# Scores of the chunked gated linear attention: seven halvings of the block in place of three quarterings, with the diagonal taken by itself

## The chip, the cores and the metric

The kernel is a single program on 1 of the cores of one Trainium2 chip. The metric is device microseconds of that core for one execution; what counts is the median over several runs. All data are 32-bit floats.

## The reference, cut to what matters

One layer of a hybrid decoder trunk over 256 tokens of width 2048. The normalised input goes through one wide projection. Three branches read it: gated linear attention (GLA), a softmax attention with a forgetting bias (FoX) and a cross-attention into 256 memory tokens. Their outputs are gated, projected, summed and projected once more. The change lies in the first branch, which has 4 heads with 128 key channels each:

```python
def step(state, inp):
    qi, ki, vi, gi = inp
    b = jnp.cumsum(gi, axis=2)
    ...
    diff = b[:, :, :, None, :] - b[:, :, None, :, :]
    decay = jnp.exp(jnp.where(causal[None, None, :, :, None], diff, -jnp.inf))
    scores = jnp.einsum('bhid,bhjd,bhijd->bhij', qi, ki, decay)
    o_intra = jnp.einsum('bhij,bhje->bhie', scores, vi)
```

A score of query i and key j is a sum over 128 channels d of q[i,d] · k[j,d] · exp(b[i,d] − b[j,d]), for j ≤ i. The decay depends on the channel, so the scores are no plain matrix product. Where a fixed token m lies between the keys and the queries, the factor splits into exp(b[i]−b[m]) · exp(b[m]−b[j]), both at most 1, and a matrix product over the channels does it.

## The kernel before, in words

**The stream of weights.** Nearly all of the work is a chain of matrix products with 2048 x 512 blocks of weights, taken in the order of the list `ORDER` (lines 39 to 46): GLA queries, keys, two value blocks, FoX queries, keys, values, memory keys, and so on to the output projection. A block comes in four loads of 1 MB on SyncE's queue (`w_load`, three buffers `raw`). ScalarE casts each eighth of a block to a rounded part `hi` (`w_cast`, L174), VectorE takes the rest `lo` = raw − `hi` (`w_sub`, L187), and TensorE multiplies by both. Of `hi` and of `lo` there are four buffers each. A block is done either as `natural` (L224 to L226: tokens on the partitions of the result, three products of 512 columns per token half and 128 rows of weights) or as `transposed` (L254 and L259: features on the partitions, groups of four products of 512 columns and four of 256, one group per 128 features and quarter of the block).

**What sets the order.** The order is written by hand. The weight stream is the backbone; everything else is written as generators that stand in three lanes (`post`, `side`, `main`). After every piece of the stream (one group in `transposed`, six products in `natural`) `pull()` lets each lane emit up to its next `yield`; `yield n` means that the next n pulls are between this stage and the next. Engines work through their own instructions in this order.

**The scores.** `gla_scores` (L590 to L723) runs in the lane `main`, beside the blocks of FoX queries, keys and values and the start of the memory keys. The 4 heads times 256 tokens stand along the free axis as 8 blocks `e` of 128 tokens, 128 channels on the partitions. `gB` holds the cumulated log decay (L575), `gqf` and `gkf` queries and keys, and `gA` the 8 score blocks of 128 x 128, which start as zeros. The products between the first 128 tokens and the last 128 (`cd`, L666) and the output (`gla_out`, L725 and on, L736, L737) stay as they are.

Inside a block of 128 tokens it goes in three levels, s = 32, 8 and 2. At a level each run of 4s tokens falls into quarters. Every key is scaled once, relative to the end of its own quarter (`prep_keys`, L612; the exponential L678; times the keys L681). For each of the three quarter ends b the queries after it are scaled relative to it (`prep_queries`, L623, three subtractions per half of the blocks; the exponential L682 or L686; `times_q`, L631). The three sets stand side by side, 96 + 64 + 32 = 192 columns per block. TensorE multiplies the 128 keys of a block with its 192 columns of queries (L707), two blocks into one PSUM bank, four such banks per level. From each bank VectorE copies three parts into `gA` under a mask (`copy_predicated`, L721). A fourth round does the pairs of neighbours (`prep_pairs`, L641, L642, L698, L647) and the diagonal: its right-hand side is 64 columns of odd queries and 128 columns of plain queries, so that the same product of 192 columns gives both. Masks are made by GpSimd at the start (`make_masks`, L494).

In numbers: 32 products of 192 columns. Two of them are emitted between two pulls, so that they stand in 16 places of TensorE's order. Tiles of 4 KB per partition (`a4`) come from a pool of 14; the scores take 11 of them in the levels.

```python
            for c in range(4):
                ps = att()[:, :2 * Q_N].rearrange("p (a b) -> p a b", a=2)
                for j in range(2):
                    e = 2 * c + j
                    MM(ps[:, j, :], lhsT=E[:, e * P:(e + 1) * P], rhs=Qs[c // 2][:, e % 4, :],
                       start=True, stop=True)
                ...
                yield 1
                for dst, mask, src in places:
                    nc.vector.copy_predicated(
                        dst, mask.bitcast(U32).unsqueeze(1).to_broadcast(list(src.shape)), src)
            yield 1
```

Of the kernel before, what the change touches and what calls it, by code (L numbers as in the profile page):

```python
# [10 lines left out]
F32 = mybir.dt.float32  # L11
F32R = mybir.dt.float32r
AF = mybir.ActivationFunctionType
ALU = mybir.AluOpType
AX = mybir.AxisListType

P = 128
# [33 lines left out]
QS = 128 ** -0.5  # L51
N_WARM = 7

STEPS = (32, 8, 2)
Q_OFF = (0, 96, 160)
Q_N = 192
BR_KT = (range(0, 8), range(8, 12), range(12, 16))


# [1 line left out]
def body(ctx, tc, xw, memT, xn, memn, wall, wsm, wup, cst, fgain, out):  # L61
    nc = tc.nc
    MM = nc.tensor.matmul

    cpool = ctx.enter_context(tc.tile_pool(name="cpool", bufs=1))
# [16 lines left out]
    def a4(shape, dt=F32):  # L82
        return apool.tile(shape, dt, tag="a4", name=nm("a"))
# [7 lines left out]
    def att():  # L91
        return ps_att.tile([P, NB], F32, tag="att", name=nm("att"))
# [232 lines left out]
    def row_of(col, row, wait=2):  # L325

        dg = a2([P, NT, P])
        for t in range(NT):
# [16 lines left out]
    ident = cpool.tile([P, P], F32, name="ident")  # L345
    ones = cpool.tile([P, P], F32, name="ones")
    nc.vector.memset(ones, 1.0)
    nc.gpsimd.affine_select(out=ident, in_=ones, pattern=[[-1, P]],
                            compare_op=ALU.is_equal, fill=0.0, base=0,
                            channel_multiplier=1)  # L350
# [136 lines left out]
        return r  # L487


    gmask = cpool.tile([P, len(STEPS), Q_N], F32, name="gmask")  # L490
    gpair = cpool.tile([P, 64], F32, name="gpair")
    fmask = cpool.tile([P, 3 * P], F32, name="fmask")

    def make_masks():  # L494

        nc.gpsimd.memset(gmask, 1.0)
        for li, s in enumerate(STEPS):
            for b in range(3):
                w, nb = (3 - b) * s, 32 // s
                mk_ = gmask[:, li, Q_OFF[b]:Q_OFF[b] + nb * w].rearrange("p (b s) -> p b s", s=w)  # L500
                nc.gpsimd.affine_select(out=mk_, in_=mk_, pattern=[[-4 * s, nb], [0, w]],
                                        compare_op=ALU.is_ge, fill=0.0, base=-b * s, channel_multiplier=1)
                nc.gpsimd.affine_select(out=mk_, in_=mk_, pattern=[[4 * s, nb], [0, w]],
                                        compare_op=ALU.is_ge, fill=0.0, base=(b + 1) * s - 1, channel_multiplier=-1)

        nc.gpsimd.affine_select(out=gpair, in_=ones[:, :64], pattern=[[-2, 64]], compare_op=ALU.is_equal,
                                fill=0.0, base=0, channel_multiplier=1)

        nc.gpsimd.memset(fmask, 0.0)
        for c in (0, 2):  # L510
            nc.gpsimd.affine_select(out=fmask[:, c * P:(c + 1) * P], in_=fmask[:, c * P:(c + 1) * P],
                                    pattern=[[-1, P]], compare_op=ALU.is_ge, fill=-1e30,
                                    base=0, channel_multiplier=1)
# [76 lines left out]
    def gla_scores():  # L590
        gB, gq, gk = G["B"], G["q"], G["k"]
        gqf, gkf = gq.rearrange("p h s -> p (h s)"), gk.rearrange("p h s -> p (h s)")
        B4 = gB.rearrange("p (h t i) -> p h t i", h=4, t=2)

        def blocks(x, half, s):

            return x[:, 512 * half:512 * half + 512].rearrange("p (b s) -> p b s", s=s)

        def of_q(Q, b, s):
            w = (3 - b) * s  # L600
            return Q[:, :, Q_OFF[b]:Q_OFF[b] + 32 * (3 - b)].rearrange("p e (b s) -> p e b s", s=w)

        def later(x, half, b, s):

            v = blocks(x, half, 4 * s)[:, :, (b + 1) * s:]
            return v.rearrange("p (e b) s -> p e b s", e=4)

        def prep_keys(s):

            E = a4([P, 1024])  # L610
            Bv = gB.rearrange("p (b s) -> p b s", s=s)
            nc.vector.tensor_tensor(out=E.rearrange("p (b s) -> p b s", s=s),  # L612
                                    in0=Bv[:, :, s - 1:s].to_broadcast([P, 1024 // s, s]), in1=Bv,
                                    op=ALU.subtract)
            return E

        def prep_queries(s, half):

            Q = a4([P, 4, Q_N])
            for b in range(3):  # L620
                w, nb = (3 - b) * s, 32 // s
                end = blocks(gB, half, 4 * s)[:, :, (b + 1) * s - 1:(b + 1) * s]
                nc.vector.tensor_tensor(  # L623
                    out=of_q(Q, b, s), in0=later(gB, half, b, s),
                    in1=end.rearrange("p (e b) s -> p e b s", e=4).to_broadcast([P, 4, nb, w]),
                    op=ALU.subtract)
            return Q

        def times_q(Q, s, half):
            for b in range(3):  # L630
                nc.vector.tensor_tensor(out=of_q(Q, b, s), in0=of_q(Q, b, s),  # L631
                                        in1=later(gqf, half, b, s), op=ALU.mult)

        def pick(v, u):
            return v[:, :, u].rearrange("p (e b) -> p e b", e=4)

        def prep_pairs(half):

            Q = a4([P, 4, Q_N])
            Bh = blocks(gB, half, 2)  # L640
            nc.vector.tensor_tensor(out=Q[:, :, :64], in0=pick(Bh, 1), in1=pick(Bh, 0), op=ALU.subtract)  # L641
            nc.scalar.copy(Q[:, :, 64:], gqf[:, 512 * half:512 * half + 512].rearrange(  # L642
                "p (e i) -> p e i", e=4))
            return Q

        def times_odd(Q, half):
            nc.vector.tensor_tensor(out=Q[:, :, :64], in0=Q[:, :, :64],  # L647
                                    in1=pick(blocks(gqf, half, 2), 1), op=ALU.mult)


        gA = G["A"] = a4([P, 8, P])
        nc.gpsimd.memset(gA, 0.0)
        U32 = mybir.dt.uint32
        cd = a4([P, 4, 2, P])
        nc.vector.tensor_tensor(out=cd[:, :, 0, :], in0=B4[:, :, 0, P - 1:P].to_broadcast([P, 4, P]),
                                in1=B4[:, :, 0, :], op=ALU.subtract)
# [7 lines left out]
        ps = att()  # L664
# [4 lines left out]
        nc.scalar.copy(gX, ps.rearrange("p (a b) -> p a b", a=4))  # L669
        yield from fox_decay()  # L670

        for li in range(len(STEPS) + 1):
            s = STEPS[li] if li < len(STEPS) else None
            Qs = []
            if s:
                E = prep_keys(s)
                yield 2
                nc.scalar.activation(E, E, AF.Exp, scale=1.0 / 16)  # L678
                Qs.append(prep_queries(s, 0))
                yield 2  # L680
                nc.vector.tensor_tensor(out=E, in0=E, in1=gkf, op=ALU.mult)  # L681
                nc.scalar.activation(Qs[0], Qs[0], AF.Exp, scale=1.0 / 16)  # L682
                yield 2
                Qs.append(prep_queries(s, 1))
                yield 2
                nc.scalar.activation(Qs[1], Qs[1], AF.Exp, scale=1.0 / 16)  # L686
                times_q(Qs[0], s, 0)
                yield 2
                times_q(Qs[1], s, 1)
                yield 2  # L690
            else:
                E = gkf
                for half in range(2):
                    Qs.append(prep_pairs(half))
                yield 2
                for half in range(2):
                    odd = Qs[half][:, :, :64]
                    nc.scalar.activation(odd, odd, AF.Exp, scale=1.0 / 16)  # L698
                yield 2
                for half in range(2):  # L700
                    times_odd(Qs[half], half)
                yield 2
            for c in range(4):
                ps = att()[:, :2 * Q_N].rearrange("p (a b) -> p a b", a=2)
                for j in range(2):
                    e = 2 * c + j
                    MM(ps[:, j, :], lhsT=E[:, e * P:(e + 1) * P], rhs=Qs[c // 2][:, e % 4, :],  # L707
                       start=True, stop=True)
                A2 = gA[:, 2 * c:2 * c + 2, :]
                if s:  # L710
                    places = [(A2.rearrange("p a (b s) -> p a b s", s=4 * s)[:, :, :, (b + 1) * s:],
                               gmask[:, li, Q_OFF[b]:Q_OFF[b] + 32 * (3 - b)].rearrange(
                                   "p (b s) -> p b s", s=(3 - b) * s),
                               ps[:, :, Q_OFF[b]:Q_OFF[b] + 32 * (3 - b)].rearrange(
                                   "p a (b s) -> p a b s", s=(3 - b) * s)) for b in range(3)]
                else:
                    places = [(A2.rearrange("p a (b s) -> p a b s", s=2)[:, :, :, 1], gpair, ps[:, :, :64]),
                              (A2, ident, ps[:, :, 64:])]
                yield 1
                for dst, mask, src in places:  # L720
                    nc.vector.copy_predicated(  # L721
                        dst, mask.bitcast(U32).unsqueeze(1).to_broadcast(list(src.shape)), src)
            yield 1  # L723

    def gla_out():  # L725
        oa = G["o"] = [a4([P, 1024]) for _ in range(NT)]
# [301 lines left out]
    for n in range(4):  # L1028
        gates = []
        for br in range(3):  # L1030
            ps = natural(x12, range(KT), w_kts(w_block()))
# [201 lines left out]
```

## Time and profile before

| | |
|---|---|
| median of 3 runs | 810.99 us (810.86 to 811.27) |
| the profiled execution | 810.85 us |
| its span, first to last instruction | 808.8 us |
| TensorE matmul busy | 799.7 us, 99% of the span |
| TensorE weight load busy | 673.5 us, 83% |
| VectorE busy | 498.3 us, 62% |
| ScalarE busy | 404.6 us, 50% |
| GpSimd busy | 23.7 us, 3% |
| first and last product of the score levels start at | 108.7 and 186 us |

The profiled execution takes 2.05 us more than its span: that is what lies before the first and after the last instruction. Busy times of TensorE are of overlapping products: a row of the trace gives an instruction's own duration, and what one costs in a stream is the distance from its start to the next one's. A matrix product of 32-bit floats stands in the trace as two loads of weights and two matmuls; the products of the weight stream, in the rounded format, as one of each. A row of the timeline merges neighbours of one line, and its time is that from the first one's start to the last one's end.

### The profile page before, as it was taken

How to read it: one execution, taken by the hardware profiler on the slowest of the kernel's cores; microseconds unless marked ns; L12 is line 12 of the kernel's file. 1: busy time of each engine (PE TensorE's matmuls, PEld its weight loads, DVE VectorE, ACT ScalarE, POOL GpSimd, SP SyncE). 2: the span in 40 equal slices, each digit the busy share in tenths (PEclk: the TensorE clock that was granted, in tenths of full speed). 3: DMA queues.
4: the chain of work that ended last, by engine and by line, in shares of the span. 5: the costliest groups of instructions: out<-in, count | busy, mean ns of one | idle time of the engine just before them, and what ended most of it. 6: DMA issues, size and time to landing. Idle time of an engine off the chain costs nothing.

```text
span 808.8 us, 9948 instructions
## 1 busy us (share of the span) xinstructions
PE 799.7 (99%) x3888; PEld 673.5 (83%) x3888; DVE 498.3 (62%) x703; ACT 404.6 (50%) x558; POOL 23.7 (3%) x44
## 2 busy tenths in 40 slices
PE   9999999999999999999999999999999999999996
PEld 8888888888888788888888888888888888888885
DVE  6767979885756566676445644465446544575653
ACT  6768655643545375565444444434443444444632
POOL 8000000100000000000000000000000000000000
PEclk9999999999999999999999999999999999999999
DMA  9945737552543444455555555555555555548633
GB/s 327 396 181 187 265 131 248 211 208 105 179 182 120 166 161 142 168 185 208 187 184 201 172 197 204 199 179 194 201 175 197 198 175 200 208 158 300 244 130 104
DMA packets 25854, 157.30 MB, mean 194 GB/s; under 512 B 3040, under 2 KB 3568, under 8 KB 8912
## 3 DMA queue, kind: packets, MB, share of 16 engines
q1 hardware_dynamic: 25536, 156.64, 54.0%
q8 instruction: 30, 0.49, 0.2%
q14 instruction: 16, 0.13, 0.0%
q10 hardware_dynamic: 144, 0.02, 0.0%
q0 software_dynamic: 128, 0.02, 0.0%
HBM read 154.55 MB, written 2.10 MB: 194 GB/s over the span
## 4 chain that ended last, share of the span: by engine, by line
PE 96%; DVE 2%; ACT 1%; issue 1%; DVEq 0%
PE acc L224 19%; PE acc L225 19%; PE acc L226 19%; PE acc L254 13%; PE acc L259 7%; PE acc L1099 4%; PE acc L1098 4%; PE acc L1097 4%; PE att L254 2%; PE att L707 1%; PE att L259 1%; DVE lo L187 1%; PE att L443 0%; PE att L1008 0%; PE att L784 0%
## 5 line engine op out<-in xcount | busy, mean ns | idle before, releaser
L187 DVE TENSOR_TENSOR lo<-raw,hi 128x1024 fp32r<-128x1024 f32 x256 | 312.1, 1222 | 201.5 <-ACT hi L174 201.3
L174 ACT CAST hi<-raw 128x1024 fp32r<-128x1024 f32 x256 | 266.4, 1052 | 322.8 <-PE acc L226 238.7
L224 PE MATMUL acc<-hi,x 128*128 128x512 f32 x544 | 214.8, 395 | 0.0
L225 PE MATMUL acc<-lo,x 128*128 128x512 f32 x544 | 212.0, 390 | 0.0
L226 PE MATMUL acc<-hi,x 128*128 128x512 f32 x544 | 211.9, 390 | 0.0
L226 PEld LDWEIGHTS acc<-hi,x 128*128 128x128 f32 x544 | 102.1, 188 | 21.7
L224 PEld LDWEIGHTS acc<-hi,x 128*128 128x128 f32 x544 | 102.2, 188 | 20.7 <-issue 0.3
L225 PEld LDWEIGHTS acc<-lo,x 128*128 128x128 f32 x544 | 102.2, 188 | 20.6 <-DVE lo L187 0.4
L254 PE MATMUL acc<-x,hi 128*128 128x512 f32 x384 | 108.0, 403 | 0.0
L254 PEld LDWEIGHTS acc<-x,hi 128*128 128x128 f32 x384 | 66.8, 189 | 9.8 <-issue 0.3
L259 PEld LDWEIGHTS acc<-x,lo 128*128 128x128 f32 x384 | 58.8, 189 | 8.2
L259 PE MATMUL acc<-x,lo 128*128 128x256 f32 x384 | 61.0, 280 | 0.0
L224 PE MATMUL acc<-hi,oT 128*128 128x512 f32 x128 | 49.8, 389 | 0.0
L225 PE MATMUL acc<-lo,oT 128*128 128x512 f32 x128 | 49.8, 389 | 0.0
L226 PE MATMUL acc<-hi,oT 128*128 128x512 f32 x128 | 49.8, 389 | 0.0
L1097 PE MATMUL acc<-hi,a 128*128 128x512 f32 x96 | 37.5, 391 | 0.0
L1099 PE MATMUL acc<-hi,a 128*128 128x512 f32 x96 | 37.4, 389 | 0.0
L1098 PE MATMUL acc<-lo,a 128*128 128x512 f32 x96 | 37.4, 389 | 0.0
L226 PEld LDWEIGHTS acc<-hi,oT 128*128 128x128 f32 x128 | 24.0, 188 | 5.0
L224 PEld LDWEIGHTS acc<-hi,oT 128*128 128x128 f32 x128 | 24.0, 188 | 5.0
L225 PEld LDWEIGHTS acc<-lo,oT 128*128 128x128 f32 x128 | 24.0, 188 | 5.0
L1099 PEld LDWEIGHTS acc<-hi,a 128*128 128x128 f32 x96 | 18.0, 188 | 3.7
(220 smaller groups left out, 770.8 us busy)
## 6 DMA issues: line engine op xcount, KB each, us to landing
raw<-wall SPq DMA_DIRECT2D x130, 1024.0 KB, 4.7
a<-xn SPq DMA_DIRECT2D x8, 512.0 KB, 8.4
xw<-xw SPq DMA_DIRECT2D x4, 768.0 KB, 7.0
xw<-xw SPq DMA_DIRECT2D x7, 384.0 KB, 5.8
a<-memT SPq DMA_DIRECT2D x4, 512.0 KB, 6.3
a<-memn SPq DMA_DIRECT2D x4, 512.0 KB, 6.1
lraw<-wall SPq DMA_DIRECT2D x2, 1024.0 KB, 7.6
out<-a SPq DMA_DIRECT2D x8, 256.0 KB, 3.1
```

The source lines that it names most:

```text
L174: nc.scalar.copy(hi, raws[q][:, 2 * s:2 * s + 2, :])
L187: nc.vector.tensor_tensor(out=lo, in0=raws[q][:, 2 * s:2 * s + 2, :], in1=parts[n][0].bitcast(F32), op=ALU.subtract)
L224: MM(ps[t], lhsT=h1, rhs=hi, start=(kt == first), stop=False)
L225: MM(ps[t], lhsT=h1, rhs=lo, start=False, stop=False)
L226: MM(ps[t], lhsT=h2, rhs=hi, start=False, stop=(kt == last))
L254: MM(ps[c], lhsT=hi[:, c * P:(c + 1) * P], rhs=h_of(h, kt).rearrange("p a s -> p (a s)"), start=(kt == 0), stop=False, skip_group_check=True)
L259: MM(ps[c][:, :S], lhsT=lo[:, c * P:(c + 1) * P], rhs=h_of(h, kt)[:, 0, :], start=False, stop=(kt == KT - 1), skip_group_check=True)
L707: MM(ps[:, j, :], lhsT=E[:, e * P:(e + 1) * P], rhs=Qs[c // 2][:, e % 4, :], start=True, stop=True)
L1097: MM(ps, lhsT=h1, rhs=hi, start=(kt == 0), stop=False)
L1098: MM(ps, lhsT=h1, rhs=lo, start=False, stop=False)
L1099: MM(ps, lhsT=h2, rhs=hi, start=False, stop=(kt == KT - 1))
```

## The change

Blocks of 2s tokens are cut in halves instead of runs of 4s in quarters, in seven levels, s = 64, 32, 16, 8, 4, 2, 1. Now a token is either a key (first half) or a query (second half) of a level, so that one tile `X` of 1024 columns holds both: in the first halves k · exp(b[m] − b), in the second q · exp(b − b[m]), with m the last token of the first half. Per level there are two subtractions of 512 columns, one exponential of 1024, two products of 512, eight matrix products (all 128 columns of the block's `X` as weights, of which those of the queries give rows that the mask drops, times the 64 query columns), all into one PSUM bank and emitted together, and one masked copy of 512 columns. The diagonal, which no level covers, is the product q · k (1024 columns), summed over the channels by eight matrix products with one column of ones, and copied under the mask of the identity.

The number of pulls stays what it was: three levels of 17 and a last round of 11 make 62, and seven levels of 8 and a last round of 6 make 62.

```diff
-STEPS = (32, 8, 2)
-Q_OFF = (0, 96, 160)
-Q_N = 192
+HALVES = (64, 32, 16, 8, 4, 2, 1)
...
-        for li in range(len(STEPS) + 1):
-            s = STEPS[li] if li < len(STEPS) else None
-            Qs = []
-            if s:
-                E = prep_keys(s)
-                yield 2
-                nc.scalar.activation(E, E, AF.Exp, scale=1.0 / 16)
-                Qs.append(prep_queries(s, 0))
-                yield 2
...
-            for c in range(4):
-                ps = att()[:, :2 * Q_N].rearrange("p (a b) -> p a b", a=2)
-                for j in range(2):
...
+        for li, s in enumerate(HALVES):
+            X = a4([P, 1024])
+            (x0, x1), (b0, b1) = halves(X, s), halves(gB, s)
+            end = b0[:, :, s - 1:s].to_broadcast([P, 512 // s, s])
+            nc.vector.tensor_tensor(out=x0, in0=end, in1=b0, op=ALU.subtract)
+            nc.vector.tensor_tensor(out=x1, in0=b1, in1=end, op=ALU.subtract)
+            yield 2
+            nc.scalar.activation(X, X, AF.Exp, scale=1.0 / 16)
+            yield 2
+            nc.vector.tensor_tensor(out=x0, in0=x0, in1=halves(gkf, s)[0], op=ALU.mult)
+            nc.vector.tensor_tensor(out=x1, in0=x1, in1=halves(gqf, s)[1], op=ALU.mult)
+            yield 2
+            ps = att().rearrange("p (e b s) -> p e b s", e=8, s=s)
+            for e in range(8):
+                MM(ps[:, e], lhsT=e_(X, e), rhs=halves(e_(X, e), s)[1], start=True, stop=True)
+            yield 1
+            dst = gA.rearrange("p e (b u s) -> p e b u s", u=2, s=s)[:, :, :, 1]
+            mask = gmask[:, li, :].bitcast(U32).rearrange("p (b s) -> p b s", s=s).unsqueeze(1)
+            nc.vector.copy_predicated(dst, mask.to_broadcast([P, 8, 64 // s, s]), ps)
+            yield 1
+
+        X = a4([P, 1024])
+        nc.vector.tensor_tensor(out=X, in0=gqf, in1=gkf, op=ALU.mult)
+        yield 3
+        ps = att()
+        for e in range(8):
+            MM(ps[:, e:e + 1], lhsT=e_(X, e), rhs=ones[:, 0:1], start=True, stop=True)
+        yield 2
+        nc.vector.copy_predicated(gA, ident.bitcast(U32).unsqueeze(1).to_broadcast([P, 8, P]),
+                                  ps[:, :8].unsqueeze(2).to_broadcast([P, 8, P]))
+        yield 1
```

The masks are made by 14 instructions on GpSimd instead of 19, and the levels take 8 tiles `a4` instead of 11.

TensorE's order in the block of FoX queries, before (`att` is a PSUM bank of the small work, `acc` one of the weight stream, `hi` and `lo` parts of weights, `x` the input; the end of a line is the result's size):

```order
L259 MATMUL acc_1050<-x_13_143,lo_1048 128x256 x2
L259 MATMUL acc_1050<-x_13_143,lo_1074 128x256 x2
L707 MATMUL att_1113<-a_984,a_962 128x192 x2
L254 MATMUL acc_1064<-x_13_143,hi_1008 128x512 x2
L254 MATMUL acc_1064<-x_13_143,hi_1034 128x512 x2
L259 MATMUL acc_1064<-x_13_143,lo_1048 128x256 x2
L259 MATMUL acc_1064<-x_13_143,lo_1074 128x256 x2
L707 MATMUL att_1127<-a_984,a_962 128x192 x2
L254 MATMUL acc_1078<-x_13_143,hi_1008 128x512 x2
```

The same block with the change, where the second level's products stand at the end of a quarter:

```order
L252 MATMUL acc_1074<-x_13_142,hi_999 128x512 x2
L252 MATMUL acc_1074<-x_13_142,hi_1030 128x512 x2
L257 MATMUL acc_1074<-x_13_142,lo_1045 128x256 x2
L257 MATMUL acc_1074<-x_13_142,lo_1070 128x256 x2
L630 MATMUL att_1131<-a_1057 128x64 x8
L252 MATMUL acc_1032<-x_28_197,hi_1084 128x512 x2
L252 MATMUL acc_1032<-x_28_197,hi_1086 128x512 x2
L257 MATMUL acc_1032<-x_28_197,lo_1096 128x256 x2
```

Two products between two groups of the stream have become eight in one place. There are seven such places, and an eighth with products of one column.

VectorE's order there, before, from the products with the queries (L631) to the first masked copy:

```order
L187 TENSOR_TENSOR lo_1048<-raw_920,hi_1008 128x1024
L631 TENSOR_TENSOR a_984<-a_984,a_109 128x4x96
L631 TENSOR_TENSOR a_984<-a_984,a_109 128x4x64
L631 TENSOR_TENSOR a_984<-a_984,a_109 128x4x32
L361 SCALAR_TENSOR_TENSOR m_112_797<-a_798,cs,m_112_797 128x256
L187 TENSOR_TENSOR lo_1074<-raw_920,hi_1034 128x1024
L631 TENSOR_TENSOR a_1028<-a_1028,a_109 128x4x96
L631 TENSOR_TENSOR a_1028<-a_1028,a_109 128x4x64
L631 TENSOR_TENSOR a_1028<-a_1028,a_109 128x4x32
L187 TENSOR_TENSOR lo_1102<-raw_968,hi_1090 128x1024
L721 COPY_PREDICATED a_848<-gmask,att_1113 128x2x96
```

With the change, one whole level on VectorE, between the copies of the first and the second:

```order
L634 COPY_PREDICATED a_842<-gmask,att_1019 128x8x64
L185 TENSOR_TENSOR lo_1045<-raw_914,hi_999 128x1024
L620 TENSOR_TENSOR a_1057<-a_819 128x16x32
L621 TENSOR_TENSOR a_1057<-a_819 128x16x32
L359 SCALAR_TENSOR_TENSOR m_112_791<-a_792,cs,m_112_791 128x256
L185 TENSOR_TENSOR lo_1070<-raw_914,hi_1030 128x1024
L185 TENSOR_TENSOR lo_1096<-raw_963,hi_1084 128x1024
L625 TENSOR_TENSOR a_1057<-a_1057,a_407 128x16x32
L626 TENSOR_TENSOR a_1057<-a_1057,a_108 128x16x32
L185 TENSOR_TENSOR lo_1117<-raw_963,hi_1086 128x1024
L359 SCALAR_TENSOR_TENSOR m_136_933<-a_934,cs,m_136_933 128x256
L634 COPY_PREDICATED a_842<-gmask,att_1131 128x16x32
```

Five instructions of a level now stand among the `lo` subtractions where there were up to 26, and one copy, of all eight products, waits for TensorE where four times three did.

## Rows read from the trace of the kernel before

**Rows 1.** The page: busy time of each engine and the granted clock in 40 slices.

```profile
PE 799.7 (99%) x3888; PEld 673.5 (83%) x3888; DVE 498.3 (62%) x703; ACT 404.6 (50%) x558; POOL 23.7 (3%) x44
...
PEclk9999999999999999999999999999999999999999
```

**Rows 2.** Stretch: length, busy PE, PEld, DVE, ACT, POOL (instructions), clock, DMA share, GB/s.

```profile
80.00:190.00 110.00, 109.88 (x579) 94.88 (x578) 93.17 (x167) 60.11 (x84) 6.04 (x8) 1.00 0.56 198
```

**Rows 3.** Waits in the same stretch: total us, times, longest.

```profile
DVE a L721 <- PE att L707: 9.3, 7, 2.5
...
PEld att L666 <- DVE a L662: 0.5, 1, 0.5
...
PEld acc L225 <- DVE lo L187: 0.4, 1, 0.4
```

**Rows 4.** Timeline of TensorE without and with products of the scores: start, us.

```profile
103.07 1.09 PE L254 MATMUL acc<-x,hi 128*128 128x512 f32 x4
...
104.48 1.09 PE L254 MATMUL acc<-x,hi 128*128 128x512 f32 x4
...
109.20 1.23 PE L254 MATMUL acc<-x,hi 128*128 128x512 f32 x4
...
110.73 0.81 PE L707 MATMUL att<-a,a 128*128 128x192 f32 x4
111.25 1.23 PE L254 MATMUL acc<-x,hi 128*128 128x512 f32 x4
```

**Rows 5.** Timeline of the weight loads around the eight of L666, 86.5 to 88.2 us.

```profile
87.04 0.97 PEld L666 LDWEIGHTS att<-a 128*128 128x128 f32 x8 [0.54 <-DVE a L662]
87.93 0.19 PEld L224 LDWEIGHTS acc<-hi,x 128*128 128x128 f32 x1
```

**Rows 6.** The matmuls of line L666: duration, ns, least, median, most.

```profile
L666 PE MATMUL att<-a x8: 275/275/377, 87.0 to 87.9; 128*128 128x128 f32 x8
```

**Rows 7.** VectorE's groups by line, 80 to 200 us: count | busy us, mean ns.

```profile
L721 DVE COPY_PREDICATED a<-gmask,att 128x192 f32<-128x192 uint32 (+2 forms) x36 | 11.1, 316 | 5.5 <-PE att L707 4.6
L631 DVE TENSOR_TENSOR a<-a,a 128x384 f32<-128x384 f32 (+2 forms) x18 | 6.5, 417 | 0.0
L623 DVE TENSOR_TENSOR a<-a 128x384 f32<-128x384 f32 (+2 forms) x18 | 6.5, 416 | 0.0
...
L612 DVE TENSOR_TENSOR a<-a 128x1024 f32<-128x1024 f32 x3 | 3.7, 1218 | 0.0
L681 DVE TENSOR_TENSOR a<-a,a 128x1024 f32<-128x1024 f32 x3 | 3.6, 1216 | 0.0
...
L721 DVE COPY_PREDICATED a<-ident,att 128x256 f32<-128x256 uint32 x4 | 1.8, 450 | 0.1
L721 DVE COPY_PREDICATED a<-gpair,att 128x128 f32<-128x128 uint32 x4 | 1.8, 448 | 4.7 <-PE att L707 4.7
...
L661 DVE TENSOR_TENSOR a<-a,a 128x512 f32<-128x512 f32 x1 | 0.7, 684 | 0.0
```

**Rows 8.** ScalarE's groups by line in the same stretch.

```profile
L678 ACT ACTIVATE a<-a 128x1024 f32<-128x1024 f32 x3 | 3.2, 1051 | 0.0
L686 ACT ACTIVATE a<-a 128x768 f32<-128x768 f32 x3 | 2.5, 846 | 0.5 <-DVE a L623 0.5
L682 ACT ACTIVATE a<-a 128x768 f32<-128x768 f32 x3 | 2.5, 837 | 0.0
```

**Rows 9.** Timelines of VectorE and of TensorE where a quarter begins.

```profile
118.06 1.22 DVE L187 TENSOR_TENSOR lo<-raw,hi 128x1024 fp32r<-128x1024 f32 x1
119.19 0.48 DVE L361 SCALAR_TENSOR_TENSOR m<-a,cs,m 128x256 fp32r<-128x256 f32 x1
...
119.68 1.09 PE L254 MATMUL acc<-x,hi 128*128 128x512 f32 x4
120.61 0.64 PE L259 MATMUL acc<-x,lo 128*128 128x256 f32 x4
```

**Rows 10.** SyncE's queue over the whole run: waits of the memory rows' loads.

```profile
SPq L315 <- DVE a L765: 5.6, 1, 5.6
```

More of the change, by code (lines that the diff above doesn't have):

```diff
@@ L487, in proj_N @@
         return r
-    gmask = cpool.tile([P, len(STEPS), Q_N], F32, name="gmask")
-    gpair = cpool.tile([P, 64], F32, name="gpair")
+    gmask = cpool.tile([P, len(HALVES), 64], F32, name="gmask")
     fmask = cpool.tile([P, 3 * P], F32, name="fmask")
@@ L496, in make_masks @@
         nc.gpsimd.memset(gmask, 1.0)
[L497 to L507, printed above, removed]
+        for li, s in enumerate(HALVES):
+            mk_ = gmask[:, li, :].rearrange("p (b s) -> p b s", s=s)
+            nc.gpsimd.affine_select(out=mk_, in_=mk_, pattern=[[-2 * s, 64 // s], [0, s]],
+                                    compare_op=ALU.is_ge, fill=0.0, base=0, channel_multiplier=1)
+            nc.gpsimd.affine_select(out=mk_, in_=mk_, pattern=[[2 * s, 64 // s], [0, s]],
+                                    compare_op=ALU.is_ge, fill=0.0, base=s - 1, channel_multiplier=-1)
         nc.gpsimd.memset(fmask, 0.0)
@@ L593, in gla_scores @@
         B4 = gB.rearrange("p (h t i) -> p h t i", h=4, t=2)
[L595 to L648, printed above, removed]
+        def halves(x, s):
+            v = x.rearrange("p (b u s) -> p b u s", u=2, s=s)
+            return v[:, :, 0], v[:, :, 1]
@@ L670, in gla_scores @@
         yield from fox_decay()
-        for li in range(len(STEPS) + 1):
-            s = STEPS[li] if li < len(STEPS) else None
-            Qs = []
-            if s:
-                E = prep_keys(s)
-                yield 2
-                nc.scalar.activation(E, E, AF.Exp, scale=1.0 / 16)
-                Qs.append(prep_queries(s, 0))
-                yield 2
[L681 to L702, printed above, removed]
-            for c in range(4):
-                ps = att()[:, :2 * Q_N].rearrange("p (a b) -> p a b", a=2)
-                for j in range(2):
[L706 to L722, printed above, removed]
-            yield 1
@@ new lines, in gla_scores @@
+        e_ = lambda x, e: x[:, e * P:(e + 1) * P]
+        for li, s in enumerate(HALVES):
+            X = a4([P, 1024])
[12 more added lines that the diff above has]
+                MM(ps[:, e], lhsT=e_(X, e), rhs=halves(e_(X, e), s)[1], start=True, stop=True)
+            yield 1
+            dst = gA.rearrange("p e (b u s) -> p e b u s", u=2, s=s)[:, :, :, 1]
+            mask = gmask[:, li, :].bitcast(U32).rearrange("p (b s) -> p b s", s=s).unsqueeze(1)
+            nc.vector.copy_predicated(dst, mask.to_broadcast([P, 8, 64 // s, s]), ps)
+            yield 1
```

## The prediction, made before the changed kernel had run

> **What bounds the kernel now.** I read the page first, for the engines over the whole run [rows 1]: TensorE is busy 99% of the span, at full clock in every slice, the others at most 62%. Since a busy TensorE can hide short waits, I then took the stretch in which the scores run, 80 to 190 us [rows 2]: TensorE 109.88 of 110.00 us busy, clock 1.00, VectorE 93 us, ScalarE 60 us. The waits of that stretch [rows 3] show what TensorE, or its weight loads, waited for: 0.5 us once and 0.4 us once, 0.9 us in 110. VectorE waits the other way round, 9.3 us in seven waits of the masked copies for the score products. So the end of the run moves by what TensorE's own instructions cost, and VectorE and ScalarE count only where they come later than TensorE needs them.
>
> **TensorE, removed.** The timeline [rows 4] gives the price of a place with two products of 192 columns. Without one, a group of the stream (L254, L259) starts 1.41 us after the group before it (103.07 to 104.48). With one, it is 2.05 us (109.20 to 111.25). The difference is 0.64 us for four trace instructions, 0.161 us each, which is what 192 columns cost. There are 16 such places in like blocks: 16 x 0.64 = 10.3 us go.
>
> **TensorE, added.** Seven levels of eight products of 64 columns, and eight of one column: 64 products, so 128 instructions, each with its own load of 128 columns of weights. The trace has no product this narrow, and the price of the instruction decides the case. If columns set it, as for the 192, a 64-column instruction costs 0.161 x 64/192 = 0.054 us and one with a single column next to nothing: 112 x 0.054 = 6.0 us. If it costs as much as a 192-column one whatever its width, it is 128 x 0.161 = 20.6 us. The nearest row is L666, eight instructions of 128 columns in a stream of the same kind, all loading 128 columns of weights [rows 5]: their first load starts at 87.04, the load of the stream's next product at 87.93, so (87.93 - 87.04)/8 = 0.111 us each. That alone doesn't say whether 128 columns or the load set it, since 128/192 of 0.161 is 0.107. But the first matmul of the eight, for which TensorE had idled, is recorded with 377 ns and the middle one with 275 [rows 6]: it had nothing to hide its load behind, and the 102 ns more are the load. A load that takes about 0.1 us by itself, and starts when the product before it starts, is not hidden by a product that streams for 0.054 us or less. I take 0.111 us for all 128, 14.2 us, as the load sets it and the load is the same.
>
> The Trainium skill, page "TensorE: Matmul & The Clock Gate", section "LDWEIGHTS (loading the stationary operand)", speaks against the change: a load takes its columns divided by 1.2 ns, whatever the rows or the moving columns, which is 107 ns for 128. The 102 ns of the row above agree. By the page's figure the sum would be 13.7 us instead of 14.2.
>
> **VectorE.** Removed, from the groups by line [rows 7]: 11.1 + 1.8 + 1.8 us of masked copies, 6.5 + 6.5 for the queries, 3.7 + 3.6 for the keys, the pairs not counted: 35.0 us. Added: 28 operations of 512 columns at 0.684 (L661), 19.2 us; the product of the diagonal, 1.22 (as L681); and eight masked copies. The copy of 256 columns took 0.450 us; the one of 128 columns that writes every other element, 0.448, so short runs cost double. Scaled up from these, which is on the high side as each has a fixed part: 512 columns 0.90 us, or 1.8 at s = 2 and 1; the last copy, 1024 columns, 1.8 us. Five times 0.9 and three times 1.8 make 9.9 us. Together 30.3 us, 4.7 less than before. Should every subtraction and product that writes runs of one or two also cost double, 8 x 0.68 = 5.5 us come on top, and it is about what it was. **ScalarE** loses 3.2 + 2.5 + 2.5 = 8.2 us [rows 8], the pairs again not counted, and gains 7 x 1.05 = 7.4 us. None of it is on the path: TensorE waits 0.9 us in all, of which 0.5 is for an operation that stays. I cost it at nothing. Its cover is the lead of VectorE over TensorE. Where a quarter of a transposed block begins, that lead is smallest: a `lo` ends at 118.06 + 1.22 = 119.28 and is first used as the third product of the group that starts at 120.61 [rows 9], some 1.5 us later.
>
> **The new wait.** A masked copy now waits for all eight products of its level, 16 x 0.111 = 1.8 us of TensorE, and behind it in VectorE's queue stand two `lo` subtractions and the next level's two subtractions, 0.90 + 2 x 1.22 + 0.48 + 2 x 0.68 = 5.2 us up to the second `lo` (0.48 for a scaling of the memory rows [rows 9]). Meanwhile TensorE has, after the eight products, a whole quarter to do: four groups of 1.41 us, and 1.1 us of the next one before that `lo` is needed, 6.7 us. So the lead is some 1.5 us, as it was. The next level's own chain has eight pulls, over 11 us.
>
> **The rest.** Masks on GpSimd: 14 instructions for 19, and all of GpSimd's 23.7 us [rows 1] would fit in the time before the first copy several times. SyncE's order of loads is the same. One load of the memory rows waited 5.6 us for a tile of the pool [rows 10] and held up the weights behind it; the levels take three tiles fewer, so I expect that wait not to grow, and nothing from it, since TensorE didn't wait. The number of pulls is the same, 62, so the work after the scores keeps its place.
>
> **The sum.** 14.2 - 10.3 = +3.9 us on TensorE, nothing else on the path. The profiled execution took 810.85 us, of which 808.8 are the span; 810.85 + 3.9 = 814.75. The median of the runs is 0.14 us above that execution, so I predict **814.9 us**. A change of less than 0.2%, 1.6 us, is what a measurement of this kernel can't tell from none.
>
> **Rivals.** *Narrow is cheap (faster).* If the load of the next weights did hide, because several can be under way at once, the column price would hold: 6.0 - 10.3 = -4.3, 806.7 us. It decides where an instruction costs less than 10.3/128 = 0.080 us. For it: weight loads overlap products everywhere in the stream. Against it: the 102 ns of rows 6. Chance 0.07.
>
> *Half-hidden (no change).* If a load began a little before the product ahead of it, the price could lie between: at the middle of 0.054 and 0.111, 0.083 us, it is 128 x 0.083 - 10.3 = +0.3, 811.3 us. The same page of the Trainium skill, section "Back-to-back issue gap", gives some 81 ns for each product of 128 columns in a sustained stream of load and product pairs, by which the sum would be +0.1 us. The 0.111 us of rows 5 at those 128 columns disagree, and the measurement decides here. Chance 0.06.
>
> *Late parts (slower still).* If masked copies, or writes to every other element, cost about double what I took, the `lo` behind a copy comes after its use, and TensorE stands. It decides from 1.5 us of extra work between a copy and the second `lo`. A miss of 0.3 to 0.9 us at each of seven levels is 2 to 6 us, so 817 to 821 us. The upper bound of the instruction's price gives the same end: 20.6 - 10.3 = +10.3, 821.3 us. For it: 9.3 us of VectorE waiting [rows 3] show that both run close. Against it: VectorE has some 5 us less to do. Chance 0.11.
>
> **Range and chances.** The forecast has 0.76. Its price may be 0.107 to 0.113 (13.7 to 14.5 us), and the 0.9 us of waits could go: 813.5 at the least; short waits for a `lo` can add some 2 us. The range is 813.3 to 817.3, with the lower part of the late parts in it. Faster by over 0.2%: 0.07; within: 0.06; slower: 0.87.
>
> **What would show it.** Right: 112 matmuls of 64 columns and 16 of one column in the trace, about 0.11 us from start to start, a level's eight products some 1.8 us longer than the groups around them; TensorE's waits in the stretch still under 2 us; VectorE some 5 us less busy. Wrong: starts 0.06 to 0.09 us apart (rivals one and two), or weight loads that wait for a `lo` (rival three).

## The result, and the profile after

The changed kernel took 814.73 us (median of 5 runs, 814.64 to 815.10), the kernel before, run beside it, 810.99 us (810.86 to 811.27). The ratio is 1.0047, with a 95% interval of 1.0036 to 1.0057: slower by 3.7 us, against a forecast of +3.9 us and 814.9 us. The profiled execution took 814.73 us and has a span of 812.8 us, 4.0 more than before.

The page of the changed kernel, engines over the whole run, answers to [rows 1]:

```profile
PE 803.1 (99%) x3952; PEld 676.8 (83%) x3952; DVE 489.5 (60%) x650; ACT 403.3 (50%) x552; POOL 21.2 (3%) x39
...
PEclk9999999999999999999999999999999999999999
```

TensorE has 64 matmuls more (64 went, 128 came, two in the trace for each product of the code), and it is still the engine that is busy 99% of the time, at full clock. VectorE lost 8.8 us and ScalarE 1.3; neither moved the end. The stretch of the scores, with the columns of [rows 2]:

```profile
80.00:190.00 110.00, 109.88 (x621) 95.33 (x619) 83.10 (x113) 57.04 (x76) 6.04 (x8) 1.00 0.55 197
```

The waits of VectorE and of TensorE's weight loads in the same stretch, which answer to [rows 3]:

```profile
DVE a L634 <- PE att L630: 15.1, 6, 4.8
...
PEld att L608 <- DVE a L604: 0.5, 1, 0.5
PEld acc L223 <- DVE lo L185: 0.4, 1, 0.4
```

TensorE idles 0.1 us there, as before, and its loads wait for the same two things as before, 0.9 us in all. What grew is VectorE's wait for the products, from 9.3 us in seven waits to 15.1 in six: it has less to do, and stands before six of the seven masked copies. The timelines of TensorE say where the time was lost, first the kernel before, then the changed one, each from the end of the same block:

```profile
100.29 1.07 PE L254 MATMUL acc<-x,hi 128*128 128x512 f32 x4
...
100.39 1.89 PE L630 MATMUL att<-a 128*128 128x64 f32 x16
```

Up to the first place of the scores the changed kernel is 0.1 us late. Behind the last one, from 190 and from 194 us on, both have 618.8 us left. So 3.9 of the 4.0 us arise between the two, where TensorE idles 0.1 us: the lost time is its own work. Its place in the timeline of TensorE, one level (L630) between groups of the stream (L252, L257), answers to [rows 4]:

```profile
111.51 0.63 PE L257 MATMUL acc<-x,lo 128*128 128x256 f32 x4
111.98 1.09 PE L252 MATMUL acc<-x,hi 128*128 128x512 f32 x4
112.91 0.64 PE L257 MATMUL acc<-x,lo 128*128 128x256 f32 x4
113.39 1.90 PE L630 MATMUL att<-a 128*128 128x64 f32 x16
115.09 1.17 PE L252 MATMUL acc<-x,hi 128*128 128x512 f32 x4
116.10 0.63 PE L257 MATMUL acc<-x,lo 128*128 128x256 f32 x4
```

From one L257 to the next it is 1.40 us without a level (111.51 to 112.91), 3.19 us with one (112.91 to 116.10): a level costs 1.79 us, 0.112 us for each of its 16 instructions. The weight loads say the same, first for the same level, then for the diagonal, whose products move one column (L642):

```profile
113.27 1.88 PEld L630 LDWEIGHTS att<-a 128*128 128x128 f32 x16
115.06 0.76 PEld L252 LDWEIGHTS acc<-x,hi 128*128 128x128 f32 x4
...
186.95 1.87 PEld L642 LDWEIGHTS att<-ones,a 128*128 128x128 f32 x16
188.74 0.76 PEld L252 LDWEIGHTS acc<-m,hi 128*128 128x128 f32 x4
```

115.06 - 113.27 and 188.74 - 186.95 are both 1.79 us. Sixteen instructions that move 64 columns and sixteen that move one take the same time, since they load the same 128 columns of weights.

### The profile page after: what moved, and what is told of

Read it like the earlier page. It is cut to its first block, busy times and chain, and to the rows that moved or that the text cites. A ratio compares the mean times of both kernels' runs of the same rounds, so it can differ in the third digit from the quotient of the medians.

```text
span 812.8 us, 10012 instructions
## 1 busy us (share of the span) xinstructions
PE 803.1 (99%) x3952; PEld 676.8 (83%) x3952; DVE 489.5 (60%) x650; ACT 403.3 (50%) x552; POOL 21.2 (3%) x39
## 4 chain that ended last, share of the span: by engine, by line
PE 95%; DVE 2%; ACT 1%; issue 1%; DMA 0%; SPq 0%; DVEq 0%
PE acc L222 19%; PE acc L224 19%; PE acc L223 19%; PE acc L252 13%; PE acc L257 7%; PE acc L1021 4%; PE acc L1020 4%; PE acc L1022 4%; PE att L252 2%; PE att L630 1%; PE att L257 1%; DVE lo L185 1%; PE att L441 0%; DMA xw<-xw 0%; PE att L931 0%
## 5 line engine op out<-in xcount | busy, mean ns | idle before, releaser
L185 DVE TENSOR_TENSOR lo<-raw,hi 128x1024 fp32r<-128x1024 f32 x256 | 312.3, 1223 | 206.0 <-ACT hi L172 205.9
L252 PE MATMUL acc<-x,hi 128*128 128x512 f32 x384 | 107.4, 401 | 0.0
L252 PEld LDWEIGHTS acc<-x,hi 128*128 128x128 f32 x384 | 66.4, 189 | 9.8 <-issue 0.3
L257 PEld LDWEIGHTS acc<-x,lo 128*128 128x128 f32 x384 | 58.8, 189 | 8.2
L257 PE MATMUL acc<-x,lo 128*128 128x256 f32 x384 | 61.0, 280 | 0.0
```

The lines of the kernel that those rows point to most:

```text
L185: nc.vector.tensor_tensor(out=lo, in0=raws[q][:, 2 * s:2 * s + 2, :], in1=parts[n][0].bitcast(F32), op=ALU.subtract)
L252: MM(ps[c], lhsT=hi[:, c * P:(c + 1) * P], rhs=h_of(h, kt).rearrange("p a s -> p (a s)"), start=(kt == 0), stop=False, skip_group_check=True)
L257: MM(ps[c][:, :S], lhsT=lo[:, c * P:(c + 1) * P], rhs=h_of(h, kt)[:, 0, :], start=False, stop=(kt == KT - 1), skip_group_check=True)
```

## The experiments

Eight kernels, in two sets; the kernel before, run beside them, stood at 810.91 us in the first set and at 810.98 in the second. The first four are edits of the changed kernel; two ask about the price of its products, two about its cover. The first of them, and the last of the eight, leave out, in the levels, the scores of the keys in the second half of each block of 128 tokens; the others compute all scores.

**Half the weights.** The price is the load's, if half the columns of weights make it half.

```diff
-                MM(ps[:, e], lhsT=e_(X, e), rhs=halves(e_(X, e), s)[1], start=True, stop=True)
+                MM(ps[:64, e], lhsT=X[:, e * P:e * P + 64], rhs=halves(e_(X, e), s)[1], start=True, stop=True)
...
-            nc.vector.copy_predicated(dst, mask.to_broadcast([P, 8, 64 // s, s]), ps)
+            nc.vector.copy_predicated(dst[:64], mask[:64].to_broadcast([64, 8, 64 // s, s]), ps[:64])
```

> As the changed kernel, but each of the 56 products of the levels takes only the first 64 tokens of its block as weights instead of all 128 (and copies 64 partitions), so that scores of the other keys are left out. Theory A (the load of the weights sets the price of a narrow product, and the load goes by its columns): an instruction falls from 0.112 us to about 0.056, 112 x 0.056 = 6.2 us less, 808.5 us. Theory B (a fixed price of some 0.11 us per instruction, whatever it loads or streams): no change, 814.7 us.

Measured: 811.19 us (810.96 to 811.73), ratio 1.0004 [0.9995, 1.0013]. That is 3.5 us under the changed kernel, of the 6.2 that theory A expected; theory B, by which nothing should move, is out. By columns alone, 64 moving ones would cost 0.054 us as well (0.161 x 64/192), so the run shows that the load's price fell to about half or below. The rest shows in the timeline of TensorE of this kernel, at the same level as above:

```profile
111.87 1.09 PE L252 MATMUL acc<-x,hi 128*128 128x512 f32 x4
112.80 0.63 PE L257 MATMUL acc<-x,lo 128*128 128x256 f32 x4
113.36 1.15 PE L630 MATMUL att<-a 128*64 128x64 f32 x16
114.43 1.20 PE L252 MATMUL acc<-x,hi 128*128 128x512 f32 x4
115.47 0.63 PE L257 MATMUL acc<-x,lo 128*128 128x256 f32 x4
```

The timeline of its weight loads there, and the durations of one, in ns, least, median and most:

```profile
113.36 1.01 PEld L630 LDWEIGHTS att<-a 128*64 128x64 f32 x16
114.43 0.76 PEld L252 LDWEIGHTS acc<-x,hi 128*128 128x128 f32 x4
...
L630 PEld LDWEIGHTS att<-a x112: 133/138/138, 100.9 to 176.5; 128*64 128x64 f32 x112
L630 PE MATMUL att<-a x112: 218/222/271, 100.9 to 176.6; 128*64 128x64 f32 x112
```

From L257 to L257 it is 2.67 us, so the level costs 1.27 instead of 1.79: 0.52 less, and seven times that are 3.6 us, which is what came. Had each instruction cost 0.056 and nothing more, it would be 0.90. The missing 0.37 us lie mostly at the two ends. The level starts 0.56 us after the L257 ahead of it (0.48 in the changed kernel). The sixteen loads start within 0.87 us (1.01 less the 0.14 of the last), 0.058 apart, but the stream's load starts 0.20 us after the last of them. And the first L252 behind takes 1.04 us up to its L257, where one without a level takes 0.93 (111.87 to 112.80) and one behind a level of the changed kernel 1.01. What delays the two ends no row names. The last experiment asks whether the price between them is so low.

**Twice the columns.** 128 moving columns instead of 64, into two banks, with two copies.

```diff
-            ps = att().rearrange("p (e b s) -> p e b s", e=8, s=s)
+            ps = [att(), att()]
             for e in range(8):
-                MM(ps[:, e], lhsT=e_(X, e), rhs=halves(e_(X, e), s)[1], start=True, stop=True)
+                MM(ps[e // 4][:, e % 4 * P:(e % 4 + 1) * P], lhsT=e_(X, e), rhs=e_(X, e), start=True, stop=True)
```

> As the changed kernel, but each product of the levels streams all 128 columns of its block instead of 64 (two PSUM banks and two masked copies per level; the result is the same). Theory A (the load sets the price; the stream of 128 columns takes no longer than the load): no change on TensorE, 814.7 us within 0.5. Theory C (a fixed part plus a price by columns, 0.054 us more for 64 more columns): 112 x 0.054 = 6.0 us more, 820.7 us.

Measured: 814.68 us (814.53 to 814.92), ratio 1.0045 [1.003, 1.006], and the same span, 812.8 us. Twice the columns cost nothing. With the one column of the diagonal this makes three widths, 1, 64 and 128, at one price.

**More between copy and `lo`.** The forecast gave VectorE a lead of some 1.5 us; here each of the two subtractions of a level is issued twice.

```diff
+            for _ in range(2):
-            nc.vector.tensor_tensor(out=x0, in0=end, in1=b0, op=ALU.subtract)
-            nc.vector.tensor_tensor(out=x1, in0=b1, in1=end, op=ALU.subtract)
+                nc.vector.tensor_tensor(out=x0, in0=end, in1=b0, op=ALU.subtract)
+                nc.vector.tensor_tensor(out=x1, in0=b1, in1=end, op=ALU.subtract)
```

> As the changed kernel, but the two subtractions of each level are done twice: 14 operations of 0.69 us, 9.6 us more on VectorE. Theory A (TensorE's own instructions set the end, VectorE's work is free as long as it stays within its lead of some 1.8 us at a quarter's start): 814.7 us within 0.5. Theory D (VectorE's lead is used up, so that its work counts): up to 9.6 us more, 824 us.

Measured: 815.61 us (815.34 to 816.14), ratio 1.0057 [1.004, 1.0074]; 0.9 us over the changed kernel, though the two intervals overlap. Of the 9.7 us more that the subtractions take (14 more at 0.69), about a tenth arrived. The waits of weight loads in the stretch show one more than in the changed kernel:

```profile
PEld acc L252 <- DVE a L242: 0.9, 1, 0.9
PEld att L608 <- DVE a L604: 0.5, 1, 0.5
PEld acc L223 <- DVE lo L185: 0.4, 1, 0.4
```

It is not a `lo` that is late. L242 is the addition that empties a bank of the stream's block, and the next block's first products (L252) wait for the bank. The forecast had watched only the `lo`.

**Far more.** Six subtractions of 512 columns into a spare tile behind each copy.

```diff
+        spare = cpool.tile([P, 512], F32, name="spare")
...
             nc.vector.copy_predicated(dst, mask.to_broadcast([P, 8, 64 // s, s]), ps)
+            for _ in range(6):
+                nc.vector.tensor_tensor(out=spare, in0=gB[:, :512], in1=gB[:, 512:], op=ALU.subtract)
```

> As the changed kernel, but six subtractions of 512 columns into a spare tile stand behind each masked copy of a level, 4.1 us of VectorE per level, 29 us in all. Theory A with its lead of about 2 us: at the five levels whose products stand in transposed blocks a rest comes some 2.1 us after its use, 5 x 2.1 = 10 us more, about 825 us, and TensorE shows waits for the rests. Theory E (VectorE never counts): 814.7 us. If all 29 us counted: 843 us.

Measured: 841.28 us (838.47 to 842.29), ratio 1.0368 [1.0347, 1.0388]: 26.5 us over the changed kernel, of some 29 that were put in (42 at 0.69). Theory A's 825 was far too low. It counted the waits and no more. The stretches of this kernel, with the columns of [rows 2], show what came on top:

```profile
80.00:220.00 140.00, 125.31 (x635) 106.91 (x634) 112.89 (x156) 56.37 (x77) 6.05 (x8) 0.91 0.45 162
...
206.00:210.00 4.00, 2.11 (x12) 1.39 (x11) 4.00 (x5) 1.58 (x2) 0.00 (x0) 0.95 0.00 0
210.00:214.00 4.00, 4.00 (x19) 4.00 (x20) 1.04 (x2) 0.00 (x0) 0.00 (x0) 0.50 0.72 262
```

TensorE idles 140 - 125.3 = 14.7 us there, which is more than the 10 of theory A. And the mean granted clock is 0.91. What that cost shows in a comparison with the changed kernel, first this one, then that, both up to where 618.8 us of the span are left:

```profile
80.00:221.70 141.70, 127.01 (x645) 108.41 (x644) 112.89 (x156) 58.06 (x79) 6.05 (x8) 0.92 0.45 160
...
80.00:194.00 114.00, 113.88 (x643) 98.87 (x642) 84.46 (x114) 58.73 (x78) 6.04 (x8) 1.00 0.55 194
```

TensorE idles 14.6 us more, and for nearly the same instructions (645 and 643) it is busy 13.1 us longer; together 27.7, by which the two spans differ (840.5 - 812.8). The mean granted clock, 8% lower over 141.7 us, accounts for some 11 of the 13.1. The two last lines of the first view show one case: TensorE was busy for 2.11 of 4.00 us, and in the 4 us behind that it had half its clock (1.2 GHz) while it was busy throughout. The weight loads of the diagonal in this kernel, their durations in ns with the first and last start:

```profile
L645 PEld LDWEIGHTS att<-ones,a x16: 330/333/333, 210.2 to 213.4; 128*128 128x128 f32 x16
```

And TensorE's waits, 80 to 220 us:

```profile
PE acc L257 <- DVE lo L185: 7.7, 4, 2.1
PE acc L252 <- DVE a L242: 3.7, 1, 3.7
PE att L631 <- DVE a L627: 2.3, 1, 2.3
PE acc L223 <- DVE lo L185: 0.7, 1, 0.7
```

Fifteen steps of the diagonal's loads from 210.2 to 213.4 are 0.21 us each, against 0.112 at full clock. Of the waits 8.4 us are for a `lo` (L185), so the rival of late parts is real once enough is put in front of a `lo`: here six subtractions, 4.1 us at each copy. The longest single wait, 3.7 us, is again for the bank that L242 empties, and 2.3 are for a level's own queries (L627); theory A had neither. That the clock fell because of the waits is read from the order of the two; no run takes the waits away and keeps the clock low.

**Versions with fewer products.** If every product costs the same up to 128 columns, the levels want to be few and wide. These three are edits of the kernel before: they keep the first levels of quarters and take the rest in one round of eight products of 128 columns, in which both factors are anchored at a token in the middle of a block, and a mask of key not after query, in the same block, keeps the part that is wanted. The pulls that they save stand behind them, so that the work after the scores keeps its place but for one pull (63 instead of 62).

```diff
-STEPS = (32, 8, 2)
+STEPS = (32, 8)
+DIAG = 8
...
+        Bv = gB.rearrange("p (b s) -> p b s", s=DIAG)
+        mid = Bv[:, :, DIAG // 2 - 1:DIAG // 2].to_broadcast([P, 1024 // DIAG, DIAG])
...
+        nc.vector.tensor_tensor(out=Kv, in0=mid, in1=Bv, op=ALU.subtract)
+        nc.vector.tensor_tensor(out=Qv, in0=Bv, in1=mid, op=ALU.subtract)
...
+                MM(ps[:, j * P:(j + 1) * P], lhsT=K[:, e * P:(e + 1) * P], rhs=Q[:, e * P:(e + 1) * P],
+                   start=True, stop=True)
```

> The kernel before with quarters of 128 and of 32 tokens as they were (s = 32 and 8), and one round in place of the third level and of the pairs: keys k exp(b_m - b_j), queries q exp(b_i - b_m) with m the middle token of a block of eight, eight products of 128 columns into two banks, copied under a mask that is one for the same block of eight and j not after i. Theory A (TensorE's instructions set the time, the larger of load and moving columns their price): 8 places of 0.64 us go, 16 instructions of 0.111 come, 1.78 - 5.15 = -3.4, so 807.5 us from 810.9. Theory W (with less score work in it, the stream itself waits, for lo subtractions or for weights from memory): half or less of that arrives, 809.2 to 810.9, with weight loads waiting for lo or issue in the stretch.

Measured: 808.56 us (808.27 to 809.77), ratio 0.9969 [0.9959, 0.9979]: 2.4 us less than before, of 3.4. The waits of weight loads in the stretch name the missing microsecond:

```profile
PEld att L711 <- DVE a L705: 1.0, 1, 1.0
```

L711 is the new round's product, L705 the multiplication of its queries. My code gave that multiplication two pulls, and VectorE ended it a microsecond late. The trace is that of the execution of 809.77 us, which also lost 1.1 us ahead of the scores, on a wait of TensorE for a part of the input (L255 for L362). The late multiplication is neither the `lo` nor the weights of theory W. The next two versions have the same two pulls and no such wait in their traces, so two pulls are enough in some places and not in this one.

```diff
-STEPS = (32, 8, 2)
+STEPS = (32,)
+DIAG = 32
```

> As the run with blocks of eight, but only the first level of quarters stays, and the last round takes blocks of 32 tokens. Theory A: 12 places of 0.64 go, 16 instructions of 0.111 come: 1.78 - 7.7 = -5.9, so 805.0 us. Theory W: half or less arrives, 808.0 to 810.9.

Measured: 805.56 us (804.75 to 806.13), ratio 0.9932 [0.9919, 0.9944]: 5.4 us less than before; the 5.9 of theory A lie inside the measured interval.

```diff
-STEPS = (32, 8, 2)
+STEPS = ()
+DIAG = 128
```

> No level at all: one round whose block is the 128 tokens, eight products of 128 columns, mask j not after i. The exponents then run to 13.1 with these inputs, since the decay is summed over up to 64 tokens to either side of the middle. Theory A: 16 places of 0.64 go, 16 instructions of 0.111 come: 1.78 - 10.3 = -8.5, so 802.4 us, and VectorE some 25 us less busy. Theory W: half or less arrives, 806.6 to 810.9, with new waits of the stream.

Measured: 802.37 us (802.24 to 802.60), ratio 0.9894 [0.9881, 0.9908]: 8.6 us less than before, where theory A said 8.5. Its page, engines over the whole run:

```profile
PE 791.0 (99%) x3840; PEld 664.4 (83%) x3840; DVE 470.9 (59%) x619; ACT 397.3 (50%) x547; POOL 14.7 (2%) x25
```

One of its two places of four products (L625) in the timeline of TensorE:

```profile
101.49 0.64 PE L260 MATMUL acc<-x,lo 128*128 128x256 f32 x4
101.96 1.06 PE L625 MATMUL att<-a,a 128*128 128x128 f32 x8
102.78 1.17 PE L255 MATMUL acc<-x,hi 128*128 128x512 f32 x4
103.79 0.63 PE L260 MATMUL acc<-x,lo 128*128 128x256 f32 x4
```

From one L260 to the next it is 2.30 us, 0.90 more than the 1.40 without a place: the 0.89 of the sum. VectorE is 27 us less busy than before, and the end moved by what TensorE lost, not by that. This version is 12.4 us faster than the changed kernel. It has a price in range: where no exponent of the kernel before is above zero, this one's go up to 13.1 with these inputs, and a decay that sums to more than about 88 over half a block would leave the range of 32-bit numbers. The block of 32 tokens keeps most of the gain and sums the decay over a quarter as many tokens.

**Half the weights, twice over.** The first experiment again, with each product issued twice in its place.

```diff
-            for e in range(8):
+            for e in 2 * tuple(range(8)):
                 MM(ps[:64, e], lhsT=X[:, e * P:e * P + 64], rhs=halves(e_(X, e), s)[1], start=True, stop=True)
```

> The run with weights of only the first 64 tokens (scores of the other keys are left out), with the eight products of each of the seven levels issued twice over in the same place. It was at 811.2 us. Theory M (an instruction with 64 columns of weights and 64 moving costs 0.056 us, and what was missing of the gain lies at the ends of a place): 112 x 0.056 = +6.3, 817.5 us. Theory G (the 8.8 us which the levels cost there, 811.2 - 600.6 - 200 = 810.9 less 10.3 plus the 1.8 of the one-column products taken from 811.2, are the price of the instructions themselves, 0.079 us each): +8.8, 820.0 us. If the hidden cost were that of whole 128-column loads after all: +12.4, 823.6 us.

(The sum in theory G reads, in order: 811.2 - (810.9 - 10.3 + 1.8) = 8.8.)

Measured: 817.21 us (816.77 to 817.70), ratio 1.0075 [1.006, 1.0091]; 112 instructions more took 6.0 us, 0.054 each. Theory M holds: within a run of them they cost half of what 128 columns of weights cost, and the rest of the first experiment is a cost at the ends of a place. The weight loads of a level show it too:

```profile
114.64 1.94 PEld L630 LDWEIGHTS att<-a 128*64 128x64 f32 x32
116.65 0.53 PEld L252 LDWEIGHTS acc<-x,hi 128*128 128x128 f32 x3
```

32 loads take 2.01 us up to the stream's, 16 took 1.07: the second sixteen cost 0.94.

## Why the prediction was right

**The bound.** TensorE was busy for 109.88 of the 110 us of the stretch before and after, and the end moved with its instructions. The version with one block shows the reverse: VectorE lost 27 us there, and the time fell by 8.6, where TensorE's sum was 8.5.

**Removed, 10.3 us.** Taken from one pair of groups. The version with one block removes all 16 places and adds 16 instructions of 128 columns; -10.3 + 1.8 = -8.5 against a measured -8.6.

**Added, 14.2 us.** The deciding step was to give an instruction of 64 columns, or of one, the price of the load, 0.111 us, read from eight instructions of 128 columns [rows 5]. It measured 0.112: eight places of 1.79 us make 14.3. The argument for the load, 102 ns on one matmul that had nothing to hide behind [rows 6], was thin, since 128 columns and 128 columns of weights came together in that row. The runs parted them: the moving columns from 1 to 128 change nothing, half the columns of weights halve the price. Its reading of the 102 ns as the load agrees with them: with 64 columns of weights the longest matmul of a level takes 271 ns and the middle one 222, 49 more; the level's first, at 113.36 us, is one of 0.27 us in the timeline. *Narrow is cheap* needed starts 0.054 us apart, *half-hidden* 0.083; the trace has 0.112, and neither is left. The section "LDWEIGHTS (loading the stationary operand)" of the Trainium skill's page "TensorE: Matmul & The Clock Gate" has a load take its columns divided by 1.2 ns; the 0.112 us at 128 and 0.054 at 64 agree in proportion, and lie within 5% of it in size.

**VectorE and ScalarE, costed at nothing.** Right, as TensorE's waits stayed at 0.9 us. The size was off on the safe side: VectorE lost 8.8 us where some 5 were forecast. The masked copies of the levels by duration, least, median and most in ns:

```profile
L634 DVE COPY_PREDICATED a<-gmask,att x7: 716/743/1322, 102.4 to 180.2; 128x512 f32<-128x512 uint32 x7
```

The timeline of VectorE at the copies of the two finest levels, s = 2 and 1:

```profile
167.04 1.32 DVE L634 COPY_PREDICATED a<-gmask,att 128x512 f32<-128x512 uint32 x1 [0.62 <-PE att L630]
...
180.21 1.32 DVE L634 COPY_PREDICATED a<-gmask,att 128x512 f32<-128x512 uint32 x1 [4.81 <-PE att L630]
```

VectorE's groups by line, for one of the subtractions and for the last copy:

```profile
L620 DVE TENSOR_TENSOR a<-a 128x512 f32<-128x512 f32 x7 | 4.8, 690 | 0.0
...
L644 DVE COPY_PREDICATED a<-ident,att 128x1024 f32<-128x1024 uint32 x1 | 1.3, 1317 | 1.7 <-PE att L642 1.7
```

Seven copies and the last took 6.3 + 1.3 = 7.6 us (the mean of the seven is 899 ns in the groups by line), not 9.9: 0.74 where 0.90 was scaled up, 1.32 where 1.8 was. That two of them, at s = 2 and 1, would cost nearly double was right. Subtractions and products at short runs were feared at double, 5.5 us; they stay at 0.69. The pairs, which were not counted, are the remainder.

**The new wait, 1.5 us of lead.** A lead of the same order was there, and the shortest that I found among the transposed blocks of the stretch is this one, first the timeline of VectorE:

```profile
131.93 1.22 DVE L185 TENSOR_TENSOR lo<-raw,hi 128x1024 fp32r<-128x1024 f32 x1
```

The timeline of TensorE at the group that uses it:

```profile
134.71 0.63 PE L257 MATMUL acc<-x,lo 128*128 128x256 f32 x4
```

The `lo` ends at 133.15 and is used as the third product of the group of 134.71, so 1.8 us later. But the step took the `lo` for the only thing that VectorE must bring in time. With 1.4 us more between copy and `lo`, the bank that L242 empties was late first. As a bound for *late parts* that made no difference, since neither happened; the price of that rival, though, took a wait at its length, and in the run with six subtractions 14.6 us more of idling went with 13.1 us by which the same work ran longer.

**The rest.** SyncE's wait of 5.6 us for a tile [rows 10] was expected not to grow; in the changed kernel the loads of the memory rows (L313) wait some 1 us in all, none of it for VectorE, and nothing followed from it.

The sum was 0.17 us high in the time, and by spans +3.9 against +4.0.

## What to carry to other kernels

When TensorE is the bound, count products by the weights that they load, not by the columns that they move: with 128 columns of weights, 1, 64 and 128 moving columns had one price here. So a scheme that halves the work in finer levels loses to a coarser one that computes and masks away more, as long as the numbers stay in range: here 8 products of 128 columns beat 32 of 192 by 8.6 us and 64 narrow ones by 12.4. Before an engine off the path is given more work, list everything that the bound engine waits for from it, the emptying of banks as well as the operands, and look at the granted clock behind long waits of TensorE: here a wait of 0.9 us, with the clock at 1.00, cost some 0.9 us, and 14.6 us more of waits cost 27.7, with the clock at 0.92.

## What had not been expected

A run of cheap products inside a stream had a cost at its ends that its own price doesn't show: 0.37 us for each place with 64 columns of weights, on top of 0.90, so that halving the load gave 3.5 of 6.2 us. Its cause is open. And in the profiled execution with six subtractions behind each copy, 14.6 us more of waiting took 27.7 us of time; the granted clock fell to 0.50 (1.2 GHz) behind a stretch of 4 us in which TensorE had been busy for 2.11.
